# A row of decays taken off GpSimd: applied per token to a residual, and on VectorE to the queries

## The chip, the cores and the metric

The kernel runs on one NeuronCore of a Trainium2 chip. TensorE (PE) multiplies matrices, VectorE (DVE) and ScalarE (ACT) work element by element, GpSimd (POOL) does a few such operations as well, and the queue of SyncE (SP) issues nearly all transfers. The metric is the device time of one execution in microseconds (us), lower is better.

## The reference, cut to what matters

A decoder trunk of two layers on 256 tokens of 1024 features. The first layer's token mixer is a gated delta rule with 8 heads of 128, the second's is causal attention; a SwiGLU feed-forward follows each. All is float32. The change lies in the delta rule alone:

```python
gc = jnp.cumsum(g.reshape(bsz, nh, n, c), -1)          # log decays, summed within a chunk
decay = jnp.where(tril, jnp.exp(gc_t - gc_s), 0.0)
rhs = concat([v_beta, k_beta * exp(gc)], -1)
u, w = triangular_solve(low, rhs)                      # low = (k_beta k^T) * decay
attn_intra = (q k^T) * decay
q_dec = q * exp(gc)
...
v_new = u_i - w_i @ state
o_i = (q_i * exp(gc)) @ state + attn_intra_i @ v_new
```

The reference takes chunks of 64 tokens; the kernel takes two chunks of 128, which gives the same function. The first chunk meets an empty state, so the factor exp(gc) on keys and queries is needed in the second chunk alone: there the kernel forms r1 = v - (k exp(gc)) S and solves with it.

## The kernel before, in words

**Main line.** TensorE runs one long line of projections. Each weight unit (128 x 1024) is loaded by the SP queue into `raw` (three buffers of two units), ScalarE rounds it to a 12-bit head `hi`, and VectorE forms the exact rest `lo = raw - hi` (`split`, L226; each unit in halves of 512 columns in the first layer). Three matmuls (hi with xTh, hi with xTl, lo with xTh) then give a nearly exact float32 product. In the first layer the order is keys (`pckeys`), queries (`pcqueries`), the gate z (`pz` of 128x512) and values (`pcvalues`, eight units of 24 matmuls), then the output projection `wo`.

**Jobs between.** All other work of the layer is written as jobs (Python generators), and a planner places their instructions between the matmuls of the main line. The planner (`Clock`, `tick`, L74 and L368) keeps an estimated time for each engine and a priority for each job, and issues what its estimates say is ready. So a changed instruction or estimate changes the order on all engines. The order is fixed when the program is built; on the chip each engine runs its own list in order.

**The block chain.** `blocks` (L848) inverts the triangular matrices: VectorE works through small products and sums in the tile `misc` (16x16 blocks, then 32x32 with the tile `wa`), with the halves of `lo` between them. The results go out to DRAM (`dX<-misc`, `dXT<-misc`) and come back rearranged (`misc<-dX`, `wa<-dXT`), all by the SP queue, which weight loads share. `doubling` (L950) then takes two steps on TensorE (`py`, `pz` of 32x32, then 64x64), and gives V. SP issues in its list's order: a load of `raw` waits there until its buffer has been split.

**The core.** `core` (L1049) runs once for each group G of four heads: pu0, u0, ps1, s1 (the state), pk = k1 S, r1 = nv - pk on VectorE, pu1, u1, then po1 = q1 S + A u1, whose result is normed, gated with z, transposed (`poT`) and split into `oTh` and `oTl` for `wo`. Each step on TensorE is followed by an evacuation on ScalarE or VectorE, which the next step waits for.

**The multiplies in question.** When the last of four `queries` jobs is done, GpSimd multiplies the second chunk's half of kT and of qT (8 heads x 128 tokens each) by the row g1 = exp(gc), two instructions of 128x1024 (`ptt`, L191; called at L1026 and L1027). `values` (L1034) waits for them in the plan.

Of the kernel before, what the change touches and what calls it, by code (L numbers as in the profile page):

```python
# [12 lines left out]
F32 = mybir.dt.float32  # L13
F32R = mybir.dt.float32r
AF = mybir.ActivationFunctionType
# [3 lines left out]
P = 128  # L19
# [34 lines left out]
class Job:  # L54
    """a line of instructions from a generator; a yield waits for all of them."""
# [18 lines left out]
class Clock:  # L74
    """estimated times of the engines; they decide the order in which work is issued, nothing else."""
# [39 lines left out]
def _first_use():  # L115
    """when each unit is first needed, in main work of the tensor engine."""
    step, f, t = 2.61, [], 0.0
    ffn = [8] + [1] * 50 + [8]
    for n in [4 if s[0] == "z" else m for s in ORDER.split() for m in ((1,) if s[0] == "z" else (1, 1))] + [8] + ffn + [8] + [1] * 16 + [8] + ffn:
        f += [t + step / 2 * k for k in range(n)]  # L120
        t += step * n
    return f
# [3 lines left out]
def trunk_kernel(ctx: ExitStack, tc: tile.TileContext, xT, xtok, wst, wgate, conv, alog, dtb,  # L126
# [15 lines left out]
    def op(eng, cost, fn, after=0.0, **kw):  # L142
        """issues an instruction of the main line; one of a job waits in its queue."""
        if ck.cur.gen is None:
            return ck.issue(ck.cur, eng, cost, fn, after, **kw)
        ck.cur.ops.append((eng, cost, fn, kw))

    def then(fn):
        """something to do when the instructions so far have been issued."""
        if ck.cur.gen is None:  # L150
            fn()
        else:
            ck.cur.ops.append((None, 0.0, fn, {}))
# [76 lines left out]
    class Stream:  # L230
# [19 lines left out]
        def first(self, s):  # L250
            """a quarter of the first chunk, then the halves of the second."""
            i, n = (0, 4) if s < 4 else (1, 2)
            if i >= self.loaded:
                self.loaded = i + 1
                self.raw[i] = wp.tile([P, 2 * UCOLS], F32, tag="raw", name=f"raw{i}", bufs=NRAW)
            c = slice(s % 4 * 2 * UCOLS // n, (s % 4 + 1) * 2 * UCOLS // n)
            nc.sync.dma_start(self.raw[i][:, c], wst[i, :, c])
            T["dma"] += 2.92 / n
            self.first_at[s] = T["dma"] + 1.0
            if i:  # L260
                self.arrive[s - 2] = self.first_at[s]

        def lead(self, u):
            """main work of the tensor engine until the unit is needed."""
            return self.first_use[u] - ck.main_pe

        def start(self):
            """when the next piece's head can start."""
            if self.piece >= len(self.pieces) or len(self.late) > 1:
                return 1e9  # L270
            u, a, b = self.pieces[self.piece]
            if u >= self.freed + NHL:
                return 1e9
            if u // 2 >= self.loaded:
                return 1e9
            return max(self.arrive[u] if u > 1 else self.first_at[2 * u + a * 2 // UCOLS], self.freet[u - NHL])
# [56 lines left out]
    def advance(j, polled):  # L333
        """runs what needs no engine at the front of a job's queue; fills the queue."""
# [71 lines left out]
    def wait(*names):  # L406
        """for a job."""
        while not all(n in done for n in names):
            yield POLL
        ck.cur.t0 = max([ck.cur.t0] + [done[n] for n in names])  # L410
# [9 lines left out]
    def until(*names):  # L420
        """for the main line."""
# [53 lines left out]
    def proj_w(ps, k0=0):  # L475
        """feature-major [128 features, 256 tokens] from one unit [128, KT, 128]."""
# [4 lines left out]
    def proj_x(ps, u, t):  # L481
        """token-major [128 tokens, 512 features] from four units [128, 2, 512]."""
# [12 lines left out]
    def acc_out(acc, ot, unit, t, first, last, cols=None):  # L495
        """token-major accumulation of one 128-row slab of an output projection."""
# [74 lines left out]
    def finish_acc(acc, names, t, row, slabs, hres, last=False):  # L571
        """the last slabs of a token tile, one half of the features after the other; then the layer norm."""
# [23 lines left out]
    ones = cst.tile([P, P], F32, name="ones")  # L596
    nc.gpsimd.memset(ones, 1.0)
    # the array's clock rises while it is busy: products of ones until the first inputs are there
# [59 lines left out]
    # ================= layer 0: gated delta rule =================  # L658
    beta = cst.tile([P, H, 2], F32, name="beta")
    e2 = cst.tile([P, H, 2], F32, name="e2")  # L660
    e2f = e2.rearrange("p h c -> p (h c)")
    bB = cst.tile([P, 16], F32, name="bB")
# [7 lines left out]
    def gates(pg):  # L670
        # the projection's four partial sums, one in each quarter of the partitions, are added as it is transposed
# [20 lines left out]
        # log(1 + e) = 2 atanh(e / (2 + e))  # L692
# [38 lines left out]
        act(e2, e2, AF.Exp)  # L731
        mark("e2")
# [19 lines left out]
    def decay(j, d1, ngc):  # L752
        """exp(gc_t - gc_s) for t >= s, for four of the heads' chunks."""
# [10 lines left out]
    def conv_silu(dst, ps, pname, ft0, name):  # L764
        """causal convolution and silu of two feature tiles."""
# [35 lines left out]
    def place(d, r, c, w=16):  # L801
        """the place [r, c] of all 32x32 blocks, 16 rows of w elements."""
# [45 lines left out]
    def blocks():  # L848
        """inverses of the 16x16 diagonal blocks, one block in each partition."""
# [22 lines left out]
        def sub(t, r, c, n, ap):  # L872
            """the element [r, c] of a 16x16 block and those at the strides `ap` from it."""
# [17 lines left out]
        def out32(q, d, r, c, src):  # L891
            """blocks of both parities or halves into the place [r, c] of their 32x32 blocks."""
# [5 lines left out]
        # 16 -> 32: one half of the columns of a block in each partition  # L898
# [40 lines left out]
    def diagonal(Xc, Vc):  # L939
        """the blocks' inverses on the diagonal."""  # L940
# [9 lines left out]
    def doubling(G):  # L950
        """block doubling 32 -> 64 -> 128 of eight inverses; X has the upper left blocks, V the transposes."""
# [52 lines left out]
    def queries(j, ps, pname):  # L1004
# [16 lines left out]
        rel(f"pa{j}")  # L1021
        mark(("q", j))
        if j == 3:
            yield from wait("nk", *[("q", i) for i in range(4)])
            g1 = big_t["grow"].rearrange("p (h c) t -> p h c t", c=2)[:, :, 1]
            ptt(kT[:, :, P:], kT[:, :, P:], g1, OP.mult)  # L1026
            ptt(qT[:, :, P:], qT[:, :, P:], g1, OP.mult)  # L1027
# [21 lines left out]
    def core(G):  # L1049
# [6 lines left out]
        def sb(name, pname, ps):  # L1056
            yield
            t = yield from t2(f"{name}{G}", (P, 4, P))
            act(t, ps)
# [3 lines left out]
        def fin(c, pname, ps):  # L1063
            """rms norm and gating of the output, which then waits to be transposed."""
# [33 lines left out]
        tt(r1, nvv[:, 1, hs], pk, OP.subtract)  # L1098
# [5 lines left out]
        u1 = yield from sb("u1", f"pu1{G}", pu)  # L1104
# [80 lines left out]
    def out_proj_norm(ot, hres, row, order, name):  # L1185
        """mixer output projection, residual and layer norm; the token tiles follow one another."""
# [113 lines left out]
    # ================= layer 1: causal attention inside the single block =================  # L1300
# [85 lines left out]
def _units(w):  # L1386
    """[k * 128, 128 * n] -> n units of 128 x (k * 128): one feature tile each."""
# [4 lines left out]
def _units_x(w):  # L1392
    """[1024, 512] -> four units of 128 x (2 * 512)."""
# [3 lines left out]
def _weights(i):  # L1397
    """all weights in the order of their use, two units of 128 x 1024 to a chunk."""
# [21 lines left out]
    # the two halves of the rotary features at partitions 0 and 32 of each head, in queries and keys alike  # L1420
# [44 lines left out]
```

## Time and profile before

| | |
|---|---|
| timed runs | 664.92, 667.39 and 672.93 us, median 667.39 |
| profiled execution, first to last instruction (span) | 664.3 us |
| TensorE busy | 644.9 us |
| VectorE busy | 431.7 us |
| ScalarE busy | 345.2 us |
| GpSimd busy | 35.4 us |

The span is what the profile gives as the profiled execution's time; what lies around it is not listed, and the fastest timed run is 0.62 us above it. TensorE is busy for 97% of the span, so time is lost only where TensorE waits. From 160 to 600 us it waits for nothing; the waits lie in the first layer and at the very end. Times in a timeline count from the first instruction. In the profile's rows fp32 matmuls of 128 columns are listed twice (a call of four shows as x8).

### The profile page before, as it was taken

To read this page: it belongs to the slowest core of one execution; us is meant where nothing else is said; L and a number is where in the kernel's file an instruction comes from. 1 tells how busy PE (TensorE), PEld (TensorE's weight loads), DVE (VectorE), ACT (ScalarE), POOL (GpSimd) and SP (SyncE) were. 2 spreads that over 40 slices of the span, in tenths; PEclk is the share of its full clock that TensorE was granted. 3 is DMA by queue.
4 is the path that set the end of the run, shared out by engine and by line. 5 is a ranking of instruction groups with operands and counts; after the bars stand their busy time and mean duration, and the time that the engine had idled before them with its cause. 6 is when DMAs were issued, how large, how long until landed. Compare 5 with 4: busy or idle time off the path is not lost.

```text
span 664.3 us, 11123 instructions
## 1 busy us (share of the span) xinstructions
PE 644.9 (97%) x4485; PEld 592.7 (89%) x4485; DVE 431.7 (65%) x703; ACT 345.2 (52%) x637; POOL 35.4 (5%) x45
## 2 busy tenths in 40 slices
PE   8999988989999999999999999999999999999995
PEld 6999868988889999999998899998889999999985
DVE  4888899267976555555548777876885555555536
ACT  4589745684564444444434468774464444444410
POOL 1051400011100000000000000000000000000001
PEclk9999999999999999999999999999999999999998
DMA  7665556535556555555553475342565555555301
GB/s 254 220 237 159 150 151 188 155 125 194 198 191 244 190 190 190 185 184 179 180 224 127 145 298 189 130 143 112 190 253 191 190 190 190 190 178 184 147 1 64
DMA packets 37172, 117.98 MB, mean 178 GB/s; under 512 B 20480, under 2 KB 21920, under 8 KB 23680
## 3 DMA queue, kind: packets, MB, share of 16 engines
q1 hardware_dynamic: 36384, 116.60, 50.9%
q8 instruction: 35, 0.57, 0.4%
q10 hardware_dynamic: 576, 0.52, 0.2%
q0 software_dynamic: 160, 0.15, 0.1%
q14 instruction: 17, 0.14, 0.1%
HBM read 115.41 MB, written 1.85 MB: 177 GB/s over the span
## 4 chain that ended last, share of the span: by engine, by line
PE 83%; issue 6%; DVE 5%; ACT 2%; DMA 2%; POOL 1%; DVEq 0%; POOLq 0%; ACTq 0%; SPq 0%
PE pf L213 31%; PE acc L213 16%; PE pqk L213 6%; PE pu L213 4%; PE bo L213 3%; PE wo L213 3%; PE pg L213 3%; PE pv L213 3%; DVE misc L172 2%; PE pl L213 2%; DVE lo L172 2%; PE po L213 2%; PE pz L213 1%; PE pcqueries L213 1%; PE pcvalues L213 1%
## 5 line engine op out<-in xcount | busy, mean ns | idle before, releaser
L172 DVE TENSOR_TENSOR lo<-raw,hi 128x1024 fp32r<-128x1024 f32 (+1 forms) x244 | 255.2, 1052 | 154.8 <-ACT hi L166 153.6
L166 ACT ACTIVATE hi<-raw 128x1024 fp32r<-128x1024 f32 (+1 forms) x244 | 219.7, 920 | 201.5 <-PE pf L213 86.7
L213 PE MATMUL pf<-xTh,hi 128*128 128x256 f32 x576 | 163.3, 284 | 0.0
L213 PE MATMUL pf<-xTl,hi 128*128 128x256 f32 x576 | 163.3, 283 | 0.0
L213 PE MATMUL pf<-xTh,lo 128*128 128x256 f32 x576 | 163.3, 283 | 0.0
L213 PEld LDWEIGHTS pf<-xTh,hi 128*128 128x128 f32 x576 | 110.6, 192 | 0.6
L213 PEld LDWEIGHTS pf<-xTl,hi 128*128 128x128 f32 x576 | 110.6, 192 | 0.6
L213 PEld LDWEIGHTS pf<-xTh,lo 128*128 128x128 f32 x576 | 110.6, 192 | 0.0
L213 PE MATMUL acc<-hi,ht 128*128 128x512 f32 x320 | 99.4, 391 | 0.0
L213 PEld LDWEIGHTS acc<-hi,ht 128*128 128x128 f32 x320 | 59.1, 188 | 11.4
L213 PE MATMUL acc<-lo,ht 128*128 128x512 f32 x160 | 62.3, 390 | 0.0
L213 PE MATMUL pqk<-xTh,hi 128*128 128x256 f32 x128 | 38.3, 299 | 0.0
L213 PE MATMUL pqk<-xTh,lo 128*128 128x256 f32 x128 | 36.2, 283 | 0.0
L213 PE MATMUL pqk<-xTl,hi 128*128 128x256 f32 x128 | 36.2, 283 | 0.0
L213 PEld LDWEIGHTS acc<-lo,ht 128*128 128x128 f32 x160 | 30.1, 188 | 6.3
L193 POOL TENSOR_TENSOR lnst<-lnst,nhalf 128x1 f32<-128x1 f32 x8 | 8.9, 1110 | 495.6 <-DVE lnst L180 495.6
L213 PEld LDWEIGHTS pqk<-xTl,hi 128*128 128x128 f32 x128 | 24.5, 192 | 0.2
L213 PEld LDWEIGHTS pqk<-xTh,hi 128*128 128x128 f32 x128 | 24.5, 191 | 0.2
L213 PEld LDWEIGHTS pqk<-xTh,lo 128*128 128x128 f32 x128 | 24.5, 191 | 0.0
L176 DVE SCALAR_TENSOR_TENSOR y<-y,lnst,gb 128x512 f32<-128x512 f32 (+1 forms) x36 | 22.8, 685 | 0.0
L213 PE MATMUL pcvalues<-xTh,hi 128*128 128x256 f32 x64 | 19.5, 304 | 0.0
L213 PE MATMUL pcvalues<-xTl,hi 128*128 128x256 f32 x64 | 18.8, 294 | 0.0
(244 smaller groups left out, 1122.6 us busy)
## 6 DMA issues: line engine op xcount, KB each, us to landing
raw<-wst SPq DMA_DIRECT2D x100, 1024.0 KB, 4.8
gb<-lnp SPq DMA_DIRECT2D x4, 1024.0 KB, 6.8
raw<-wst SPq DMA_DIRECT2D x4, 256.0 KB, 6.5
raw<-wst SPq DMA_DIRECT2D x2, 512.0 KB, 8.0
grow<-d SPq DMA_DIRECT2D x4, 256.0 KB, 6.2
y<-xtok SPq DMA_DIRECT2D x1, 1024.0 KB, 4.6
xraw<-xT SPq DMA_DIRECT2D x3, 256.0 KB, 5.1
out_dram<-y ACTq DMA_DIRECT2D x4, 128.0 KB, 1.8
```

The lines of the kernel that those rows point to most:

```text
L166: return op("act", cost, lambda: nc.scalar.activation(out_, in_, func, **kw), after)
L172: return dve(out_, 0.06 + 0.00105 * width(out_), lambda: nc.vector.tensor_tensor(out_, a, b, op=alu), after)
L176: lambda: nc.vector.scalar_tensor_tensor(out_, a, s, b, op0=op0, op1=op1), **kw)
L193: op("pool", cost, lambda: nc.gpsimd.tensor_tensor(out_, a, b, op=alu))
L213: op("pe", cost, lambda: nc.tensor.matmul(out_, lhs, rhs, start=start, stop=stop))
```

## The change

GpSimd's two multiplies are gone. For the queries, each `queries` job multiplies the second-chunk half of its own two heads by the same row on VectorE (128 x 2 x 128, four instructions in all). For the keys, kT stays as it is, so pk lacks the factor; the factor of a token is one number per partition there (`eg`, a new tile of 128x8, made by one more exponential in `gates`), and r1 becomes pk * eg - nv, head by head: four `scalar_tensor_tensor` of 128x128 in place of one subtraction of 128x512, per group. r1 so has the opposite sign, and the evacuation of u1 turns it back with scale -1.

```diff
+    eg = cst.tile([P, H], F32, name="eg")
...
         act(e2, e2, AF.Exp)
+        act(eg, ngc.rearrange("p (h c) -> p h c", c=2)[:, :, 1], AF.Exp, scale=-1.0)
...
         tt(aT[:, 4 * j:4 * j + 4], pa, big_t["dT"][:, 4 * j:4 * j + 4], OP.mult)
         rel(f"pa{j}")
+        g1 = big_t["grow"].rearrange("p (h c) t -> p h c t", c=2)[:, 2 * j:2 * j + 2, 1]
+        q1 = qT[:, 2 * j:2 * j + 2, P:]
+        tt(q1, q1, g1, OP.mult)
         mark(("q", j))
         if j == 3:
             yield from wait("nk", *[("q", i) for i in range(4)])
-            g1 = big_t["grow"].rearrange("p (h c) t -> p h c t", c=2)[:, :, 1]
-            ptt(kT[:, :, P:], kT[:, :, P:], g1, OP.mult)
-            ptt(qT[:, :, P:], qT[:, :, P:], g1, OP.mult)
             ts(eq, ssq, 1e-6, 128.0 * 1e-6, OP.add, OP.mult)
             mark("q")
...
-        def sb(name, pname, ps):
+        def sb(name, pname, ps, **kw):
             yield
             t = yield from t2(f"{name}{G}", (P, 4, P))
-            act(t, ps)
+            act(t, ps, **kw)
...
         r1 = yield from t2(f"r1{G}", (P, 4, P))
-        tt(r1, nvv[:, 1, hs], pk, OP.subtract)
+
+        for i in range(4):
+            stt(r1[:, i], pk[:, i], eg[:, 4 * G + i:4 * G + i + 1], nvv[:, 1, 4 * G + i], OP.mult, OP.subtract)
...
-        u1 = yield from sb("u1", f"pu1{G}", pu)
+        u1 = yield from sb("u1", f"pu1{G}", pu, scale=-1.0)
```

Because the planner's estimates changed, the order moved on every engine from the z projection to the start of `wo`. The first place is VectorE's list in the block chain, around the end of the 16x16 inversion (`dT<-pa` are a queries job's attention products). Before:

```order
L172 TENSOR_TENSOR dT<-pa_1068,dT 128x512
L189 TENSOR_REDUCE misc<-misc 128x2x7
L172 TENSOR_TENSOR lo_1107<-raw_822,hi_1106 128x512
L172 TENSOR_TENSOR misc<-misc 128x512
L189 TENSOR_REDUCE ones<-misc 128x64
L172 TENSOR_TENSOR lo_1122<-raw_965,hi_1121 128x512
L172 TENSOR_TENSOR misc<-misc,ones 128x512
L189 TENSOR_REDUCE misc<-misc 128x8x8
L172 TENSOR_TENSOR lo_1122<-raw_965,hi_1121 128x512
L172 TENSOR_TENSOR misc<-misc,cB 128x256
L172 TENSOR_TENSOR lo_1151<-raw_965,hi_1150 128x512
L183 COPY misc<-misc 128x256
```

With the change:

```order
L172 TENSOR_TENSOR misc<-misc 128x98
L172 TENSOR_TENSOR qT<-qT,grow 128x2x128
L189 TENSOR_REDUCE misc<-misc 128x2x7
L172 TENSOR_TENSOR lo_1125<-raw_968,hi_1124 128x512
L172 TENSOR_TENSOR misc<-misc 128x512
L189 TENSOR_REDUCE ones<-misc 128x64
L172 TENSOR_TENSOR misc<-misc,ones 128x512
L189 TENSOR_REDUCE misc<-misc 128x8x8
L172 TENSOR_TENSOR misc<-misc,cB 128x256
L183 COPY misc<-misc 128x256
L172 TENSOR_TENSOR lo_1125<-raw_968,hi_1124 128x512
L172 TENSOR_TENSOR lo_1151<-raw_968,hi_1150 128x512
```

A query multiply now stands in the chain, and two halves of `lo` that stood between its steps stand behind them. From the chain's first step (`cB`) to the step after this piece (`misc<-l`, the first of the 32x32 blocks) there are 9 halves of `lo` before and 7 with the change, and three of the four query multiplies.

The second place is SP's list around the second round trip of the blocks through DRAM. Before:

```order
L248 DMA raw_1199<-wst 128x2048
L248 DMA raw_1247<-wst 128x2048
L248 DMA raw_1316<-wst 128x2048
L224 DMA dX<-misc 64x16x8 x2
L224 DMA dXT<-misc 64x8x16 x2
L248 DMA raw_1397<-wst 128x2048
L224 DMA misc<-dX 128x16x32
L224 DMA wa<-dXT 128x16x32
```

With the change:

```order
L248 DMA raw_1205<-wst 128x2048
L248 DMA raw_1259<-wst 128x2048
L224 DMA dX<-misc 64x16x8 x2
L224 DMA dXT<-misc 64x8x16 x2
L248 DMA raw_1333<-wst 128x2048
L224 DMA misc<-dX 128x16x32
L224 DMA wa<-dXT 128x16x32
L248 DMA raw_1376<-wst 128x2048
```

One weight load fewer stands ahead of the stores `dX` and `dXT`; one still stands between the stores and the loads that bring the blocks back.

The third place is TensorE's list in the core of the first group, from pu1 on. Before (the four heads' po1 alternate):

```order
L216 MATMUL ptv_1782<-ident,vt_1731 128x128 x4
L213 MATMUL pu_1796<-r_1770,V 128x128 x4
L213 MATMUL pu_1806<-nv,V 128x128 x2
L213 MATMUL po_1808<-s_1743,qT 128x128
...
L213 MATMUL po_1808<-u_1801,dT 128x128
...
L213 MATMUL ps_1828<-u_1816,misc 128x128 x4
L216 MATMUL poT_1847<-ident,zz 128x128 x4
L213 MATMUL po_1835<-u_1816,dT 128x128 x4
L213 MATMUL pk_1857<-s_1833,kT 128x128 x4
```

With the change:

```order
L213 MATMUL pcvalues_1619<-xTh,lo_1385 128x256
L213 MATMUL pu_1774<-r_1740,V 128x128 x4
L213 MATMUL po_1797<-s_1717,qT 128x128
L213 MATMUL po_1797<-u_1782,dT 128x128
...
L216 MATMUL poT_1824<-ident,zz 128x128 x4
L213 MATMUL wo_1844<-hi_1416,oTh 128x512
L213 MATMUL wo_1844<-hi_1416,oTl 128x512
L213 MATMUL wo_1844<-lo_1417,oTh 128x512
```

Before, the second group's core ran beside the first's, after all of the value projection. Now the first group's core lies between value matmuls, the second's between the first 24 matmuls of `wo`. Of the 192 value matmuls 144 stood ahead of the first `py` before, and 111 do now; the first transpose of values (`ptv`) stood ahead of `py`, after value matmul 117, and now comes after it.

## Rows read from the trace of the kernel before

**Rows 1.** The page: the span, then the busy time of TensorE.

```profile
span 664.3 us, 11123 instructions
...
PE 644.9 (97%) x4485; PEld 592.7 (89%) x4485; DVE 431.7 (65%) x703; ACT 345.2 (52%) x637; POOL 35.4 (5%) x45
```

**Rows 2.** Waits of TensorE: us in total, times, longest.

```profile
PE ptv L216 <- ACT vt L166: 3.4, 2, 2.8
PE pz L213 <- DVE lo L172: 2.4, 2, 1.4
...
PE pu L213 <- DVE r L172: 0.8, 1, 0.8
PE ps L213 <- ACT u L166: 0.7, 1, 0.7
PE py L213 <- DMA misc<-dX: 0.4, 1, 0.4
```

**Rows 3.** Stretches: length, busy PE, PEld, DVE, ACT, POOL, granted clock, DMA, GB/s.

```profile
80.00:95.90 15.90, 13.52 (x56) 9.99 (x55) 15.76 (x20) 6.80 (x14) 3.55 (x2) 1.00 0.52 146
...
112.86:116.56 3.70, 3.70 (x19) 3.70 (x20) 3.70 (x9) 3.16 (x8) 0.00 (x0) 0.57 0.87 289
...
134.41:152.00 17.59, 15.41 (x131) 14.46 (x129) 11.24 (x29) 14.31 (x49) 3.42 (x3) 1.00 0.49 179
```

**Rows 4.** Timeline of GpSimd: start, us, the instruction.

```profile
78.27 2.48 POOL L193 TENSOR_TENSOR kT<-kT,grow 128x1024 f32<-128x1024 f32 x1
80.70 2.85 POOL L193 TENSOR_TENSOR qT<-qT,grow 128x1024 f32<-128x1024 f32 x1
```

**Rows 5.** Timeline of VectorE in the block chain.

```profile
67.25 0.69 DVE L172 TENSOR_TENSOR lo<-raw,hi 128x512 fp32r<-128x512 f32 x1 [0.87 <-ACT hi L166]
...
74.01 0.69 DVE L172 TENSOR_TENSOR dT<-pa,dT 128x512 f32<-128x512 f32 x1 [0.35 <-PE pa L213]
...
78.39 0.68 DVE L172 TENSOR_TENSOR dT<-pa,dT 128x512 f32<-128x512 f32 x1
...
79.15 2.13 DVE L172 TENSOR_TENSOR lo<-raw,hi 128x512 fp32r<-128x512 f32 x1
81.21 3.27 DVE L172 TENSOR_TENSOR misc<-misc 128x512 f32<-128x512 f32 x1
...
85.12 0.68 DVE L172 TENSOR_TENSOR lo<-raw,hi 128x512 fp32r<-128x512 f32 x1
85.72 1.14 DVE L172 TENSOR_TENSOR misc<-misc,ones 128x512 f32<-128x512 f32 x1
...
88.10 0.42 DVE L172 TENSOR_TENSOR misc<-misc,cB 128x256 f32<-128x256 f32 x1
88.43 0.68 DVE L172 TENSOR_TENSOR lo<-raw,hi 128x512 fp32r<-128x512 f32 x1
...
105.25 0.69 DVE L189 TENSOR_REDUCE misc<-misc 128x32 f32<-128x512 f32 x1
```

**Rows 6.** Timeline of TensorE: the last half of z, first values, `ptv`, `py`, the feed-forward's start.

```profile
90.06 0.51 PE L213 MATMUL pz<-lo,xTh 128*128 128x512 f32 x1
...
95.91 0.28 PE L213 MATMUL pcvalues<-xTh,hi 128*128 128x256 f32 x1
...
96.86 0.28 PE L213 MATMUL pcvalues<-xTh,lo 128*128 128x256 f32 x1
...
112.86 0.70 PE L216 MATMUL ptv<-ident,vt 128*128 128x128 f32 x4 [2.76 <-ACT vt L166]
...
118.66 2.11 PE L213 MATMUL py<-misc,gdT 32*32 32x32 f32 x64 [0.42 <-DMA misc<-dX]
...
175.78 0.39 PE L213 MATMUL pg<-hi,xTh 128*128 128x512 f32 x1
```

**Rows 7.** SP's issues, by start and us: the blocks' two round trips.

```profile
88.59 1.33 SPq L224 DMA_DIRECT2D dX<-misc  x2
...
107.37 3.54 SPq L224 DMA_DIRECT2D dXT<-misc  x2
111.03 0.54 SPq L248 DMA_DIRECT2D raw<-wst  x1
```

**Rows 8.** The chain that ended last: the transfers between the blocks and `py`.

```profile
106.61 5.52 DMA dX<-misc
...
112.61 6.01 DMA misc<-dX
```

**Rows 9.** Transfers by issue: count, KB, us to landing (first the first round trip).

```profile
dX<-misc SPq DMA_DIRECT2D x2, 64.0 KB, 3.2
```

**Rows 10.** Costs of steps of the core: ScalarE's timeline (first row), then VectorE's.

```profile
150.42 0.69 ACT L166 ACTIVATE oTh<-poT,ng 128x512 fp32r<-128x512 f32 x1
...
139.65 0.69 DVE L172 TENSOR_TENSOR r<-nv,pk 128x512 f32<-128x512 f32 x1
...
141.92 1.13 DVE L176 SCALAR_TENSOR_TENSOR zz<-po,ms,zz 128x128 f32<-128x128 f32 x4 [0.92 <-POOL ms L193]
...
151.14 0.75 DVE L176 SCALAR_TENSOR_TENSOR oTl<-poT,ng,oTh 128x512 fp32r<-128x512 f32 x1 [0.93 <-ACT oTh L166]
```

## The prediction, made before the change was run

> **What bounds the kernel now.** I read the page first: TensorE is busy for 644.9 of 664.3 us [rows 1], so a change pays only where TensorE waits. The list of its waits then shows that those of the first layer between 80 and 160 us are seven: two of 2.4 together for `lo` in the z projection, 2.76 at a `ptv` and 0.7 at another, 0.42 at `py`, 0.7 for u0 and 0.8 for r1 [rows 2, 6]. The reader should see in the stretches how they divide: z (80 to 95.9) loses 15.90 - 13.52 = 2.4, the core (134.4 to 152) 17.59 - 15.41 = 2.2. After the 2.76 at `ptv` there is a stretch of 3.70 with a granted clock of 0.57, nearly half of full speed, in which TensorE counts as busy [rows 3]; it did in it what takes 0.57 x 3.70 = 2.1 otherwise, so the slow clock cost 1.6.
>
> **What the multiplies cost.** GpSimd works on kT from 78.27 to 80.75 and on qT from 80.70 to 83.55. In just this time two instructions of VectorE are long: a `lo` half that starts at 79.15 takes 2.13 where a later one of the same shape takes 0.68, and a product of 512 columns that starts at 81.21 takes 3.27 where the like one at 85.72 takes 1.14. Both end shortly after a GpSimd instruction has ended. The `dT` at 78.39, which reads one operand from PSUM, takes its usual 0.68 beside GpSimd [rows 4, 5]. So GpSimd's multiplies held VectorE up by 1.45 + 2.13 = 3.58 us, in the block chain, where each step waits for the last.
>
> **The block chain with the change.** That 3.58 goes. Two fewer halves of `lo` stand in the chain before its step `misc<-l`; a half takes 0.60 from its start to the next (85.12 to 85.72), so 1.20 goes. Three query multiplies of 256 columns come in; the like row is `misc<-misc,cB`, 0.42 long and 0.33 to the next start (88.10 to 88.43) [rows 5]. One of them falls into the 0.35 that VectorE waited for `pa` before the `dT` at 74.01, the two others cost 0.68 together. The fourth, ahead of the chain, falls into the 0.87 before the `lo` at 67.25 [rows 5]. Where a covering `lo` has gone, the next step waits for the whole of its predecessor's 0.69 and not for 0.60; some four such places cost 0.35. Sum: -3.58 - 1.20 + 0.68 + 0.35 = **-3.75** for the last reduction, which started at 105.25 and will at 101.5.
>
> One rule speaks against this step. The Trainium skill (Perfetto Trace Analysis, Optimizing Scalar/DVE Operations) says that offloading from a saturated VectorE to ScalarE or GpSimd may make sense, and warns that it might not help with GpSimd because of a port that both share. VectorE is saturated here, 15.76 of 15.90 us [rows 3], and the change puts work back on it. The rows decide for the warning: 0.68 comes back and 3.58 goes. What the first half of the rule would make of the time is rival D.
>
> **z.** TensorE's last wait for `lo` in z ended at 90.06 [rows 6]. In the new order this half stands behind `misc<-l` (a product of 512, 1.2) and its reduction, and by the steps above it is done at 89.4 instead of 90.0: z ends 0.6 earlier, at 95.3. The waits stay, two halves that were early being late now.
>
> **The way to `py`.** SP issues `dX` when the last reduction is done, at 102.2 where it was 105.94 (105.25 + 0.69). The second of these stores took 5.52 to land with a weight load just ahead of it; in the first round trip, with none in flight, a pair took 3.2 [rows 8, 9]. The third weight load is now behind, so I take 3.2 from 102.9: 106.1. SP itself needs 1.33 each for `dX` and `dXT` and 0.54 for the load between [rows 7], and is done at 105.4. Then `misc<-dX`, 6.0 as before, as a load still goes just ahead [rows 8]: `py` can start at **112.2** instead of 118.66. Ends: 111.0 if the load interferes less, 114.4 if `dXT` takes 3.54 as it did [rows 7].
>
> TensorE is there sooner. From 95.3 it has 111 value matmuls at 0.12 each (eight from 95.91 to 96.86 [rows 6]) and stands at 108.6, having no `ptv` to wait for. It waits 3.6, and I expect the slow clock behind this wait as behind the 2.76, at the same 1.6. At 118.66 the old order had 33 more matmuls and a `ptv` behind it, 33 x 0.12 and 0.4 for the `ptv` (0.70 at the clock of 0.57 [rows 3, 6]), 4.4. So 112.2 + 4.4 + 1.6 = 118.2 against 118.66: **-0.4**. The lead of 3.75 is spent in one wait.
>
> **The core.** r1 becomes four instructions; the like row is the run of four `zz<-po`, 1.13, against 0.69 for the one, so each group pays up to 0.44 [rows 10], less what a head gains by starting early: pu1's first head needs r1's first alone, after about 0.3. I count nothing and keep 0.44 as the upper end. The sign in u1 and the small `eg` cost nothing: the first is in an instruction that stands there anyway, the second runs while TensorE is in the key projection. What moves more is the order. Before, two groups side by side gave each other cover. Now the first has value matmuls as cover up to pu1, but then po1 follows pu1 at once and waits for u1 (0.7, as the row for u0), and `wo` follows `poT` at once and waits for oTh and oTl, 0.69 + 0.75 [rows 2, 10]. The second group repeats both and waits for r1 (0.8): 2 x 0.7 + 2 x 1.44 + 0.8 = 5.1. Against 2.2 before that is **+2.9**. The lower end is that cover holds everywhere, -2.2. I take the upper end, since the new list shows the consumer directly behind its producer in four of the five places.
>
> **Sum.** -0.4 + 2.9 = +2.5 on a span of 664.3: 666.8. The fastest run lies 0.6 above the span, so **667.4** for a run. That is the median of the runs (667.39), which itself lies 3.1 above the profiled span: no change that a measurement can tell. About 2%, 13.3 us, is what a measurement of this kernel can tell from no change.
>
> From 160 to 600 us nothing is expected: the instructions there are the same, and TensorE waited for none of them.
>
> **Rivals.**
> A, the forecast, 0.50: the lead of the block chain ends in the wait before `py`, the core gains new gaps; 664 to 670.
> B, faster, 0.27: the value matmuls and the 24 of `wo` between the steps do cover ScalarE and VectorE, and the core's 2.2 go: 664.3 - 0.4 - 2.2 = 661.7, a run 662.3; with the load out of `misc<-dX`'s way 1.2 less, 661.1. For it speaks that 33 more matmuls are left to mix in; against it the last excerpt of TensorE's list.
> C, slower, 0.17: the wait before `py` grows. If `dXT` holds SP for 3.54 again, `py` starts at 114.4 and the wait is 5.8; decided once it is over 5, it costs 2.2 itself and, if the slow clock lasts in proportion to the wait, another 1: 667.4 + 3.2 = 670.6, to 671.5 with both groups' 0.44. Against it: no load is just ahead of the stores.
> D, 0.06: the rule's first half. If what slowed VectorE in these 5 us was not GpSimd, the 3.58 stays and the work is merely moved onto a full engine. The chain ends 3.58 later than I say, `py` at 115.8, z as much later by 2 or so; 667.4 + 3.6 = 671.0. It would be that the change doesn't do what it can do; the rows of GpSimd and VectorE ending together speak against it.
>
> **Numbers.** 667.4; A's range takes half, B and most of C with the spread of runs widen it to 662 to 672. Over 2% faster (654.0) needs more than all waits between 80 and 160 us (7.7) and the slow clock (1.6) to vanish: 0.02. Over 2% slower (680.7) needs 13 more us of waits in a part of 80: 0.03. Within: 0.95.
>
> **What would show it.** Right: no GpSimd `TENSOR_TENSOR` on kT and qT, the `lo` and the 512-column product at 0.7 and 1.2; `dX` issued near 102; a wait at `py` of 3 to 4 us with a granted clock near half after it; waits at po1 for u1 and at `wo` for oTh or oTl; the first `pg` of the feed-forward 1 to 4 us after the 175.78 of before [rows 6]. Wrong: `py` starting without a wait, a core without gaps, or VectorE still slow at that place.

## The result and the profile after

The changed kernel takes 672.28 us (median of 20 executions, 670.3 to 678.4); the kernel before took 668.13 in the same comparison. The ratio is 1.0061, 95% interval 1.0036 to 1.0087: slower by 0.6%, some 4 us, where no difference had been forecast. The median lies 0.28 us above the forecast range. Three executions stand far off the rest (709.72 us of the kernel before, 1293.9 and 2245.75 in two of the later runs); the ranges given here leave them out.

The page, to be held against [rows 1]:

```profile
span 671.6 us, 11129 instructions
...
PE 649.2 (97%) x4485; PEld 596.0 (89%) x4485; DVE 430.5 (64%) x713; ACT 345.2 (51%) x638; POOL 30.6 (5%) x43
```

This execution took 673.32 us in all, 1.7 more than its span. The span grew by 7.3 us. TensorE has no more matmuls than before, yet 4.3 us more of busy time: that is not work but a slower clock. The other 3.0 are waits. TensorE's list of waits (us in total, times, longest), to be held against [rows 2]:

```profile
PE py L213 <- DMA misc<-dX: 3.9, 1, 3.9
PE wo L213 <- ACT oTh L166: 1.8, 2, 0.9
PE po L213 <- ACT u L166: 1.4, 2, 0.8
PE pz L213 <- DVE lo L172: 1.3, 2, 0.9
...
PE pu L213 <- DVE r L176: 1.1, 1, 1.1
```

The `ptv` wait of 2.76 is gone and `py` has one of 3.9; the core waits for u, for oTh and for r. VectorE's timeline (start, us, instruction) answers to [rows 5]:

```profile
79.76 0.42 DVE L172 TENSOR_TENSOR qT<-qT,grow 128x256 f32<-128x256 f32 x1
...
80.26 0.68 DVE L172 TENSOR_TENSOR lo<-raw,hi 128x512 fp32r<-128x512 f32 x1
80.86 1.05 DVE L172 TENSOR_TENSOR misc<-misc 128x512 f32<-128x512 f32 x1
...
101.15 0.69 DVE L189 TENSOR_REDUCE misc<-misc 128x32 f32<-128x512 f32 x1
```

The `lo` half and the 512-column product that took 2.13 and 3.27 are back at 0.68 and 1.05, and the block chain's last reduction comes at 101.15 instead of 105.25. SP's issues, to be held against [rows 7], and TensorE's timeline, against [rows 6]:

```profile
101.87 1.30 SPq L224 DMA_DIRECT2D dX<-misc  x2
103.27 1.30 SPq L224 DMA_DIRECT2D dXT<-misc  x2
104.69 0.54 SPq L248 DMA_DIRECT2D raw<-wst  x1
105.34 0.38 SPq L224 DMA_DIRECT2D misc<-dX  x1
```

```profile
112.32 3.43 PE L213 MATMUL py<-misc,gdT 32*32 32x32 f32 x64 [3.90 <-DMA misc<-dX]
...
182.59 0.39 PE L213 MATMUL pg<-hi,xTh 128*128 128x512 f32 x1
```

`py` starts 6.3 us sooner and takes 3.43 instead of 2.11. The first product of the feed-forward, which was at 175.78, is 6.8 later. The stretches between show where it went (columns as in [rows 3]; the clock is the third number from the end):

```profile
112.32:120.40 8.08, 8.08 (x93) 7.79 (x94) 3.43 (x8) 5.82 (x11) 0.00 (x0) 0.50 0.71 258
120.40:127.00 6.60, 6.53 (x126) 6.10 (x125) 1.28 (x3) 4.62 (x14) 0.00 (x0) 0.98 0.01 2
127.00:131.00 4.00, 4.00 (x25) 3.71 (x24) 0.84 (x2) 1.43 (x5) 0.00 (x0) 0.57 0.51 164
...
143.00:165.00 22.00, 17.14 (x113) 14.32 (x112) 14.70 (x36) 14.31 (x46) 2.09 (x3) 1.00 0.63 237
```

For 8.08 us behind the wait TensorE ran at half of full speed, 1.2 instead of 2.4 GHz, without a gap, and for most of the 4.00 from 127 again, this time with no wait ahead of it. In the core, 143 to 165, it idles 22.00 - 17.14 = 4.9 us.

The same division can be made for every kernel below. I cut the time from 80 us to the first `pg` into stretches of half a microsecond. In each, length minus busy time is **idle**, and busy time x (1 - granted clock) is **lost to the clock**; their sums, in us, of one profiled execution each:

| kernel | first `pg` | idle | lost to the clock | ratio to before (95%) | median clock of all executions |
|---|---|---|---|---|---|
| before | 175.8 | 7.8 | 1.7 | 1 | 0.990 to 0.993 |
| the change | 182.6 | 10.5 | 5.9 | 1.0061 (1.0036 to 1.0087) | 0.989 |
| the change, again | 179.9 | 10.2 | 3.2 | 1.0071 (1.0033 to 1.0108) | 0.989 |
| change, old order | 172.7 | 7.2 | 0.0 | 0.9936 (0.9902 to 0.9971) | 0.993 |
| change, old order, again | 173.5 | 7.2 | 1.7 | 0.9967 (0.9933 to 1.0001) | 0.993 |
| old instructions, new order | 186.8 | 11.6 | 8.4 | 1.0098 (1.0065 to 1.0132) | 0.987 |
| change, wait filled, large products | 180.4 | 6.8 + 3.7 fill | 3.4 | 1.0013 (0.998 to 1.0046) | 0.995 |
| the same, again | 178.4 | 6.8 + 3.7 fill | 1.7 | 1.002 (0.9992 to 1.0047) | 0.997 |
| change, wait filled, small products | 180.2 | 6.7 + 3.7 fill | 3.4 | 1.0062 (1.0039 to 1.0086) | 0.989 |

So the change adds 2.4 to 2.7 us of idle time, and 1.5 to 4.2 of slow clock, depending on the execution. Both are held against one execution of the kernel before, whose mean clock of 0.994 lies above its medians of 0.990 to 0.993. By the medians of the last column an estimate for the typical execution is smaller: 0.001 to 0.004 of some 649 us of busy time, 0.6 to 2.6 us. The idle time is then about as large a part of the 4 us as the clock, or a larger one. The first `pg` also holds what lies ahead of 80 us, where idle time differs by up to 1.3 us from execution to execution (4.0 in the profile of before, 2.8 to 3.9 in the others).

### The profile page after: what moved, and what is told of

Its sections match the earlier page's. It is cut to its first block, busy times and chain, and to the rows that moved or that the text cites. A ratio compares the mean times of both kernels' runs of the same rounds, so it can differ in the third digit from the quotient of the medians.

```text
span 671.6 us, 11129 instructions
## 1 busy us (share of the span) xinstructions
PE 649.2 (97%) x4485; PEld 596.0 (89%) x4485; DVE 430.5 (64%) x713; ACT 345.2 (51%) x638; POOL 30.6 (5%) x43
## 3 DMA queue, kind: packets, MB, share of 16 engines
HBM read 115.41 MB, written 1.85 MB: 175 GB/s over the span
## 4 chain that ended last, share of the span: by engine, by line
PE 83%; issue 6%; DVE 6%; ACT 2%; DMA 1%; POOL 1%; DVEq 0%; POOLq 0%; ACTq 0%; SPq 0%
PE pf L213 31%; PE acc L213 16%; PE pqk L213 6%; PE pu L213 4%; PE bo L213 3%; PE wo L213 3%; PE pg L213 3%; PE pv L213 3%; DVE lo L172 2%; PE pl L213 2%; PE pcvalues L213 2%; DVE misc L172 2%; PE pz L213 1%; PE po L213 1%; PE pcqueries L213 1%
## 5 line engine op out<-in xcount | busy, mean ns | idle before, releaser
L213 PE MATMUL pcvalues<-xTh,lo 128*128 128x256 f32 x64 | 19.5, 305 | 0.0
```

The source lines that it names most:

```text
L213: op("pe", cost, lambda: nc.tensor.matmul(out_, lhs, rhs, start=start, stop=stop))
```

## The experiments

**1. The change in the old order.** The first theory was that not the changed instructions but the order they bring costs the time. This kernel has all of the change's instructions, with the planner's estimates of the kernel before: TensorE, ScalarE and SP issue in the old order, and VectorE differs only by the new instructions.

```diff
-        act(eg, ngc.rearrange("p (h c) -> p h c", c=2)[:, :, 1], AF.Exp, scale=-1.0)
+        op("act", 0.0, lambda: nc.scalar.activation(eg, ngc.rearrange("p (h c) -> p h c", c=2)[:, :, 1], AF.Exp, scale=-1.0))
...
-        tt(q1, q1, g1, OP.mult)
+        then(lambda: nc.vector.tensor_tensor(q1, q1, g1, op=OP.mult))
...
+            for _ in range(2):
+                op("pool", 0.15 + 0.0021 * 1024, lambda: None)
...
-        for i in range(4):
-            stt(r1[:, i], pk[:, i], eg[:, 4 * G + i:4 * G + i + 1], nvv[:, 1, 4 * G + i], OP.mult, OP.subtract)
...
+        dve(r1, 0.06 + 0.00105 * 512, form)
```

The exponential for `eg` and the queries' multiplies cost the plan nothing, GpSimd's two estimates stay without an instruction behind them, and `form` issues the four operations of r1 as one of 512 columns in the plan.

> All instructions of the change, issued on TensorE, ScalarE and SyncE in the order of the kernel before. Theory 1, that the loss is the new order's doing (py ahead of the queries' products, so that TensorE stands still 3.9 us in front of py and runs at half clock behind it): the end of the block chain comes about 4 us earlier as in the change, py starts near 116.2 instead of 118.66, the time is 2 to 3 us below the kernel before, a ratio near 0.996, and the stretch behind py has a clock above 0.9. Theory 2, that the changed instructions themselves cost it (four multiplies and four short operations more on VectorE, the sign on ScalarE, the gaps in the core): 1 to 4 us above the kernel before, a ratio of 1.002 to 1.006, with the first gate product 3 to 7 us later than at 175.78.

It takes 663.89 us; the ratio to before is 0.9936 (0.9902 to 0.9971). TensorE's two waits in this stretch, and the stretch around them:

```profile
PE ptv L216 <- ACT vt L166: 3.5, 2, 2.8
PE py L213 <- DMA misc<-dX: 1.8, 1, 1.8
```

```profile
109.33:117.10 7.77, 5.93 (x95) 5.68 (x95) 5.16 (x11) 4.93 (x11) 0.00 (x0) 1.00 1.12 277
```

`py` starts at 115.06, the clock is full, and the first `pg` stands at 172.7. Theory 1 held and theory 2 fell: the same instructions gain time in one order and lose it in the other. A part of the gain lies where the prediction expected none: the two waits of z for `lo`, 2.4 us [rows 2], are missing from this run's list of waits. Against that `py` waits longer (1.8 against 0.4). Once more on another chip:

> The run in the old order once more, on the same chip as the next one. It was 0.64% below the kernel before (0.29 to 0.98). If that holds, the ratio is again 0.990 to 0.997, the median 663 to 665, and no execution has a mean clock below 0.988. If the first run was a lucky draw of clocks, the ratio is 0.997 or more and executions at 0.98 are among them.

The ratio was 0.9967 (0.9933 to 1.0001), the median 664.93. The gain is about half the size, with an interval that just reaches 1, so this run alone doesn't show it; one execution had a mean clock of 0.981. What can be said: 0 to 1% under the kernel before, and clearly under the change in both cases, whose intervals begin at 1.0033 and above.

**2. The old instructions in the new order.** The mirror of the first: GpSimd's two multiplies and the single subtraction, planned with the change's estimates.

```diff
-        tt(q1, q1, g1, OP.mult)
+        dve(q1, 0.06 + 0.00105 * 256, lambda: None)
...
+            for w in (kT, qT):
+                then(lambda w=w: nc.gpsimd.tensor_tensor(w[:, :, P:], w[:, :, P:], row, op=OP.mult))
...
-            stt(r1[:, i], pk[:, i], eg[:, 4 * G + i:4 * G + i + 1], nvv[:, 1, 4 * G + i], OP.mult, OP.subtract)
+            dve(r1[:, i], 0.12 + 0.00105 * 128,
+                lambda i=i: i == 0 and nc.vector.tensor_tensor(r1, nvv[:, 1, hs], pk, op=OP.subtract))
...
-        u1 = yield from sb("u1", f"pu1{G}", pu, scale=-1.0)
+        u1 = yield from sb("u1", f"pu1{G}", pu)
```

> The instructions of the kernel before (both multiplies on GpSimd, the rest r1 as one subtraction) in the order of the changed kernel. Theory 1 (order and clock): VectorE is locked again while GpSimd multiplies, so py starts near 115 to 116, the wait in front of it grows from 3.9 to about 7 us, half clock behind it; the time is 2 to 4 us above the changed kernel, 6 to 8 us above the kernel before, a ratio of 1.009 to 1.012. Theory 2 (the instructions): within 2 us of the kernel before, a ratio of 0.997 to 1.003.

675.52 us, 1.0098 (1.0065 to 1.0132): the slowest of all, as theory 1 had it. VectorE's timeline at the multiplies, and TensorE at `py`:

```profile
79.44 2.74 DVE L172 TENSOR_TENSOR lo<-raw,hi 128x512 fp32r<-128x512 f32 x1
82.10 2.52 DVE L172 TENSOR_TENSOR misc<-misc 128x98 f32<-128x98 f32 x1
```

```profile
117.75 3.02 PE L213 MATMUL py<-misc,gdT 32*32 32x32 f32 x64 [2.87 <-DMA misc<-dX]
```

Even a product of 98 columns, 0.33 long in the change, takes 2.52 beside GpSimd. `py` comes 5.4 later than in the change. Two things went against the forecast: `py` starts at 117.75, not at 115 to 116, and the wait before it is 2.87, not 7. Another wait of 4.0 had come up in z, for `lo`, with products of 512 columns behind it:

```profile
90.53 0.50 PE L213 MATMUL pz<-lo,xTh 128*128 128x512 f32 x1 [4.00 <-DVE lo L172]
```

```profile
91.00:98.00 7.00, 6.69 (x17) 4.35 (x16) 6.90 (x12) 5.19 (x10) 0.00 (x0) 0.51 0.79 185
```

So behind this wait TensorE ran at half clock for 7.0 us, with one more wait of 0.31 in them and without a single small product.

**3. The multiplies left out.** The kernel before, in its own order, without GpSimd's two multiplies and with nothing in their place; the second chunk's keys and queries lack their factor.

```diff
-            ptt(kT[:, :, P:], kT[:, :, P:], g1, OP.mult)
-            ptt(qT[:, :, P:], qT[:, :, P:], g1, OP.mult)
+            for _ in range(2):
+                op("pool", 0.15 + 0.0021 * 1024, lambda: None)
```

> The kernel before in its own order, with GpSimd's two multiplies left out and nothing in their place (the second chunk's keys and queries lack the decay factor). It measures the lock of VectorE alone. If the lock is on the path to py: lo at 79 us takes 0.68 instead of 2.13, the 512-column operation at 81 us 1.1 instead of 3.27, the block chain's last reduction is 3 to 4 us earlier, py follows at about 116 instead of 118.66, the time 2 to 3 us below the kernel before, a ratio near 0.996. If the lock is hidden by the wait for the stream or the transfers: the time is within 0.5 us of the kernel before, a ratio of 0.999 to 1.001.

664.79 us, 0.9952 (0.9917 to 0.9987). VectorE:

```profile
78.73 1.06 DVE L172 TENSOR_TENSOR misc<-misc 128x512 f32<-128x512 f32 x1
80.42 0.68 DVE L172 TENSOR_TENSOR lo<-raw,hi 128x512 fp32r<-128x512 f32 x1
...
100.48 0.69 DVE L189 TENSOR_REDUCE misc<-misc 128x32 f32<-128x512 f32 x1
```

The last reduction is 4.8 earlier than in [rows 5], and `py` follows at 113.82, both more than I had expected of the lock. z's two waits for `lo` are gone here too. Removing the lock alone is worth about 3 us in the old order (by the interval 1 to 6). By its times the change in the old order can't be told from this run. By its waits it can: with nothing put in the multiplies' place `py` comes 1.2 earlier (113.82 against 115.06), and TensorE idles 5.2 us between 80 us and the first `pg` against 7.2. So the added VectorE work costs some 2 us of waiting in the old order, which the spread of the times hides.

**4. Which estimate turns the order.** The changed kernel with one line changed: the queries' multiplies cost the plan nothing.

```diff
-        tt(q1, q1, g1, OP.mult)
+        then(lambda: nc.vector.tensor_tensor(q1, q1, g1, op=OP.mult))
```

> The changed kernel with one difference: the four multiplies of the queries on VectorE count nothing in the planner's estimates. TensorE's rows are then those of the kernel before up to the recurrence, and in the recurrence (29 rows) they differ from it as r1's four operations make them. It splits what the order costs. Theory 1 (the query multiplies' estimate alone turns the front around): the front is as in the run in the old order (first values product of the transposes near 109, py near 115, no wait of 3.9 us), the recurrence has the waits of the changed kernel (4 to 5 us instead of 2.2), so the time is 2 to 3 us above the run in the old order, 1 to 2 us below the kernel before, a ratio of 0.996 to 0.999. Rival (the order of the recurrence is the larger part): the time is 4 us or more above the run in the old order, a ratio of 1.000 or more.

667.0 us, 1.0008 (0.9967 to 1.0049). TensorE's waits in front of the values and of `py`:

```profile
109.09 1.11 PE L216 MATMUL ptv<-ident,vt 128*128 128x128 f32 x4 [2.79 <-ACT vt L166]
115.10 2.11 PE L213 MATMUL py<-misc,gdT 32*32 32x32 f32 x64 [0.78 <-DMA misc<-dX]
```

The front has turned back, by one estimate of a third of a microsecond, four times. The GpSimd estimates that the change takes away are not needed for that: this kernel lacks them as well. The core did not do as I said: I counted on its waits of the changed kernel, 4 to 5 us, and it has 0.69 + 0.68 + 0.28 + 1.99 = 3.6 (for u0, vt, u1 and r1), against 2.2 before. So a part of the change's core waits, 4.9 - 3.6 = 1.3, comes with the front's order. Five executions in a group 6 us above the others left the comparison with the old order open, so both ran again on one chip:

> The run with the queries' multiplies at no cost to the planner once more. Its 12 executions fell into seven of 664.6 to 668.0 (clock 0.991 to 0.994) and five of 672.0 to 674.5 (0.981). If the order of the recurrence costs by its waits, the lower group again stands 1 to 2 us above the old order's run and the upper group is rare or missing. If it is the clock that the order of the recurrence makes worse, a third or more of the executions is again at 0.981 and 8 us longer.

0.997 (0.9943 to 0.9996), beside 0.9967 for the old order, and no execution at 0.981. The upper group is gone, as the first half of the expectation had it. Whether the rest stands above the old order is not settled: by the medians it does, by 1.1 us (666.00 against 664.93), by the ratios hardly at all, and the idle sums are 7.2 in both. Most of the order's cost lies in the front.

**5. The wait filled.** Sixteen products of the identity go ahead of `py`, into columns of its bank that nothing uses; all else is the change.

```diff
+        def keep():
+            for _ in range(16):
+                nc.tensor.matmul(pb[:, 256:384], ident, ident, start=True, stop=True)
+            nc.tensor.matmul(py[32:64, 0], gdT[0:32, 0, 32:64], Xc[0:32, 0], start=True, stop=True)
...
+                if G == b == i == 0:
+                    op("pe", 0.0014 * 32, keep)
+                    continue
```

> The changed kernel with 16 products of the identity with itself (128x128, into unused columns of the bank) ahead of the first py product, so that TensorE is busy in the wait for the blocks' inverses; the order is otherwise the changed kernel's. Theory 1a (the half clock behind the wait is what costs): no stretch at half clock from 112 to 122, py ends its products as early as the data lets it, the first gate product 3 to 6 us earlier than at 182.59, the time 3 to 6 us below the changed kernel, about 667 to 669, a ratio to the kernel before of 0.995 to 1.000. Theory 1b (the waits and the gaps cost, the clock comes back by itself at the same moment): within 1 us of the changed kernel, a ratio of 1.005 to 1.008 to the kernel before.

668.91 us, 1.0013 (0.998 to 1.0046): 0.5% less than the change, and a median clock of 0.995 instead of 0.989. TensorE's timeline and two stretches behind it:

```profile
108.26 3.73 PE L961 MATMUL py<-ident 128*128 128x128 f32 x32
112.25 0.24 PE L962 MATMUL py<-misc,gdT 32*32 32x32 f32 x2 [0.26 <-DMA misc<-dX]
```

```profile
112.25:115.38 3.13, 3.13 (x72) 3.09 (x73) 3.13 (x8) 3.04 (x6) 0.00 (x0) 0.98 1.04 336
115.38:118.50 3.12, 3.12 (x31) 2.90 (x30) 0.31 (x1) 2.80 (x6) 0.00 (x0) 0.50 0.84 344
```

`py` now runs at full speed. But a half-clock stretch came all the same, at 115.38, with no wait of over 0.3 us ahead of it. So a part of theory 1a fell: a wait directly ahead is not the only thing that brings the slow clock. The traces of all runs up to experiment 6 and of experiment 8 hold eight such stretches with no wait directly ahead; each stands just behind a run of 32x32 or 64x64 products (here `py`, 112.3 to 114.3). In two of the eight a wait stands ahead of those products (1.85 us in the old order's second run, 0.69 in the second run of experiment 4). And such a run does not always bring it: the kernel before and the first run of the old order issue the same products, with full clock behind all of them.

**6. The change once more**, for the slow stretches.

> The changed kernel as it is, profiled once more on the same chip as the others of this call. If the half clock belongs to the place in the program, the two stretches (112 to 121 and 127 to 131 us) come again at 0.5, and the time is 670 to 674. If the second stretch was chance, it is missing or stands elsewhere; the first, behind the wait of 3.9 us, should come again in either case.

672.04 us, 1.0071 (1.0033 to 1.0108). One row answers: of the first stretch

```profile
111.91:118.31 6.40, 6.40 (x78) 6.34 (x79) 3.27 (x8) 5.52 (x11) 0.00 (x0) 0.50 0.98 337
```

and of the second nothing, from 118.5 on the clock is full. The first belongs to the place, the second comes in some executions.

**7. Large or small products in the wait.** The test of what the eight stretches suggested: the same time in the same wait is filled with 32x32 products instead of 128x128.

```diff
-            for _ in range(16):
-                nc.tensor.matmul(pb[:, 256:384], ident, ident, start=True, stop=True)
+            for _ in range(56):
+                nc.tensor.matmul(pb[32:64, 256:288], ident[0:32, 0:32], ident[0:32, 0:32], start=True, stop=True)
```

> The run that fills the wait in front of py, with the 16 products of 128x128 replaced by 56 of 32x32 (as py's own), which by py's rows take as long (112 listed rows of 0.033 us, 3.7 us). TensorE counts as busy in the wait in both. In eight stretches of the traces so far TensorE went to half clock without any wait, each time just behind a run of 32x32 or 64x64 products. If small products count little for the clock: the fill doesn't hold it, py and what follows run at half clock as in the changed kernel, the mean clock of the executions has its median at 0.987 to 0.990, the time is 671 to 673, a ratio of 1.005 to 1.008. If being busy is enough: as the run with large products, a median clock of 0.994 or more, 668 to 670, a ratio near 1.001.

> The run with the 16 large products once more, as the control on the same chip: a median clock of 0.994 or more, 667 to 670, a ratio of 0.998 to 1.004. If the clock of 0.995 was chance, it is at 0.989 and 671 to 673 here.

With small products 671.79 us, 1.0062 (1.0039 to 1.0086), as the change without any fill; with large ones 668.87, 1.002 (0.9992 to 1.0047). The mean clocks of the executions do not overlap: 0.987 to 0.992 with small, 0.994 to 0.998 with large. TensorE with the small fill, and then the stretch behind the wait with small and with large:

```profile
108.07 3.73 PE L961 MATMUL py<-ident 32*32 32x32 f32 x112
111.97 0.24 PE L962 MATMUL py<-misc,gdT 32*32 32x32 f32 x2 [0.17 <-DMA misc<-dX]
112.05 3.24 PE L213 MATMUL py<-misc,gdT 32*32 32x32 f32 x62
```

```profile
111.97:118.90 6.93, 6.93 (x81) 6.87 (x82) 3.42 (x8) 5.81 (x11) 0.00 (x0) 0.51 0.83 304
```

```profile
111.97:118.90 6.93, 6.93 (x127) 6.67 (x123) 3.08 (x7) 5.47 (x10) 0.00 (x0) 0.75 0.77 299
```

Both fills keep TensorE busy by the profile for 3.73 us in the wait. Behind the small ones it runs at half clock for nearly all of the 6.93 us and issues 81 matmuls in them; behind the large ones it issues 127, and half clock comes only behind `py`, from 114.2 to 117.6. So for the granted clock a stretch of small products was here no better than a stretch of waiting. What about them matters is not shown: it may be how little of the array they use, or pauses between them that the profile, which models the ends of matmuls, does not show.

**8. The old order with its waits filled**, ten large products ahead of the first `ptv`, seven ahead of `py`, as a candidate for the best version.

> The run in the old order with the waits filled: ten products of the identity ahead of the first transposes of the values (wait 2.78 us) and seven ahead of the first py product (wait 1.84 us). Theory 1a (half clock behind a wait costs a part of the executions): the mean clock of the executions rises from a median of 0.993 to 0.996 or more, the time is 1 to 2 us below the run in the old order, about 662, a ratio of 0.990 to 0.993 to the kernel before. Theory 1b (the clock follows its own course): the mean clock stays at 0.993 and the time within 0.5 us of the run in the old order.

664.23 us, 0.9951 (0.9919 to 0.9983): not apart from the old order alone, and the median clock rose only from 0.993 to 0.9945. The waits are filled (idle 3.5 instead of 7.2), but the fill takes their time, and one slow stretch came again, behind `pz`:

```profile
122.50:126.10 3.60, 3.60 (x22) 3.38 (x23) 1.75 (x4) 1.34 (x4) 0.00 (x0) 0.53 0.02 5
```

Theory 1a's 1 to 2 us did not come. So theory 1b fits as well. In the old order's two profiles no slow stretch stands directly behind these waits, so there was little to buy. The best version is the change in the old order, as it is: no slower, and simpler.

## Why the prediction was wrong

**The lock of VectorE by GpSimd: right.** 3.58 us were to go, and the two instructions are back at their usual length. Rival D, that something else had slowed VectorE, is out: experiment 2 brings the slowness back with the multiplies alone, experiment 3 takes it away. In the rows each of the two long instructions ends shortly after the GpSimd instruction beside which it started [rows 4, 5]. The Trainium skill (SBUF — State Buffer, Who interferes with whom) calls the port pair that both engines share an exclusive lock, and says that a VectorE instruction with two SBUF inputs contends with a GpSimd instruction that reads SBUF, while one with at most one such input does not. The rows agree, down to the `dT` with one operand in PSUM that is not held up [rows 5].

**The way to `py`: right.** The last reduction was forecast for 101.5 and came at 101.15; z was to end at 95.3 and the first value matmul starts at 94.95; `py` was forecast for 112.2 with a wait of 3.6 and came at 112.32 with 3.90. With the 4.4 us of work that now stand behind `py`, this part alone is a gain of 118.66 - 112.32 - 4.4 = 1.9 us.

**The core: right in size, only partly in reason.** Forecast +2.9, measured 4.9 against 2.2. The four pieces of r1 were counted at nothing, with 0.44 as the upper end. In the second group they cost the upper end: pu1 waits 1.06 for r in the change and 0.55 in experiment 2, which has the same order and one subtraction. In the first group no wait for r shows in either.

**The failed step: the price of the slow clock.** "I expect the slow clock behind this wait as behind the 2.76, at the same 1.6." As the kernel before loses 1.7 to the clock too, the forecast put the change's cost in clock at nothing. The loss was 5.9 in the profiled execution and 3.2 in the second, where the first stretch alone stands. The sum closes with it: -1.9 + 2.7 + 5.9 = +6.7, measured 6.8 to the first `pg`. Filling the wait with large products gives back 0.4 to 0.5%, about 3 us of the 4 that the change costs. But the filled kernel's clock (0.995 and 0.997) is higher than that of the kernel before, so not all of these 3 us had been lost by the change.

The row that I priced by differs in two things. The wait was shorter, 2.76 against 3.90, and behind it stood a `ptv` and large value products [rows 3], where the half clock ended after 3.70 us; behind the 3.90 stands `py`, 64 products of 32x32, and the half clock lasted 6.4 to 8.1 us. Either could be the reason. Experiment 7 shows that such products, in place of the wait, do no more for the clock than waiting, and in experiment 2 a wait of 2.87 with `py` behind it was followed by half clock to about 125.2, some 7 us. But the wait of 4.00 in z of experiment 2 had large products behind it, and half clock for 7.0 us all the same. So no run separates the two for the change's own wait. My rival C had a part of it, a price in proportion to the wait (1.6 x 3.9 / 2.76 = 2.3), and that is still short.

**A second one: the base.** I took 0.6 us, the fastest run above a span from another execution. Every execution of the runs here lies 1.7 above its own span. That alone is 1.1 us: by my own terms the run should have read 668.5. And the profiled execution was a fast one of its kernel: 664.3 + 1.7 = 666.0, where the median in the comparison was 668.13. Of the 4.9 us between 667.4 and 672.28 these two make up 1.1 + 2.1; only 1.7 lie in the change itself, forecast at +2.5 and measured at 4.2 by the medians. That 1.7 is about what the slow clock cost beyond its price in the second profile (3.2 - 1.6). A span and a time may be subtracted only if they are of one execution, and a difference worked out on one execution says nothing of where the median lies.

What stays open, besides that: why some executions have a second slow stretch and others of the same kernel do not, and why a wait of 2.78 had full clock behind it in one profile of the old order and 2.79 in experiment 4 had half clock (the row of 109.09, 1.11 long where 0.66 is usual). Of the six profiles with a wait of 2.5 to 2.8 at that place, four show half clock within 1.2 us behind it and two, both of the change in the old order, do not.

## What to carry to other kernels

When a planner sets the order, a change is two changes: the instructions, and the order that their estimates bring. Build each alone, the new instructions in the old order and the old in the new; here the first gained 0.3 to 0.6%, the second lost 1%, and the change itself showed neither. When a wait of TensorE is moved, look at how long it gets and at what is issued right behind it: behind 2.76 us with large products the clock was back after 3.7 us here, behind 3.7 to 3.9 us with small ones after 6.4 to 8.1, and behind 4.0 us with large ones after 7. And do not price a stretch at slow clock by another wait's row unless both the length and the work that follows are alike.

## What the hardware showed that I had not expected

TensorE can be busy by the profile, without a gap, and still be at half clock next: 3.73 us of 32x32 products left it at 0.51 for 6.9 us, 3.73 us of 128x128 products at 0.75 (experiment 7), and eight stretches at half clock followed runs of 32x32 or 64x64 products with no wait directly ahead. The Trainium skill (TensorE: Matmul & The Clock Gate, What's actually happening) says that the clock follows how busy TensorE has been; by these rows the profile's busy time alone is not the measure of that.

One kernel's executions differ in this. The change has mean clocks from 0.977 to 0.992 and times from 670.3 to 678.4 us, lower clock with longer time, and its two profiles hold two slow stretches and one. So a price read from a single profile is that of one execution.
